# Value weights at group borders on GpSimd's DMA queue, in another order of steps; first-layer weight measures begun one block later and in other pieces

## The chip, the cores and the metric

The kernel runs on one core of a Trainium2 chip. Work that matters here is done by TensorE (PE in the profile; its weight loads are PEld), VectorE (DVE), ScalarE (ACT), GpSimd (POOL) and by DMAs, which SyncE's queue (SPq) or GpSimd's queue (POOLq) issues. Each engine works through its own list of instructions in order, and waits at an instruction until the semaphores that it needs have come. The metric is the device time of the kernel in microseconds (us), the median of several runs. The kernel's list of instructions for each engine is made by a scheduler that simulates the program on a time line while it is built: an instruction can be placed earlier than it stands in the source if its inputs are ready there, and `tc.issue_after(x)` keeps it from being placed ahead of `x`.

## What is computed

Two layers on a (1, 1024, 1024) float32 input. Layer 0 is an RG-LRU mixer (width 1536, in 12 blocks of 128), layer 1 a forgetting attention (16 heads of 64). Cut to what matters:

```python
x = x + lru_mixer(rms_norm(x, norm_g[0]), ...)
x = x + fox_mixer(rms_norm(x, norm_g[1]), fox_w_in, fox_b_f, fox_w_out)
return rms_norm(x, final_g)

def fox_mixer(h, w_in, b_f, w_out):
    u = h @ w_in                      # q, k, v, gate, forget logits
    cum = cumsum(log_sigmoid(f_logit + b_f))
    p = softmax(q k^T / 8 + cum_q - cum_k, causal)
    o = p @ v
    return (o * silu(gate)) @ w_out
```

## The kernel before

Matrix products are made of three passes with operands that are split into a high and a low part (fp32r in layer 0, fp16 in layer 1). Layer 1's fp16 parts need scales, so the squared norms of layer 1's weights have to be known before layer 1 begins. They are measured during layer 0.

**Layer 0** is the loop over 12 blocks (lines 472 to 524). A block `n` makes the input product `ups` of block n (lines 480 and 493), the gates of block n-1 (`gates`), the convolution (`conv`, DVE), the output products of earlier blocks (`project_out`, `fill`), the gate product `gps` of block n-1 (lines 511 to 516) and the recurrence (`recur`). The weights of `ups` and `gps` come through `weights`: SP loads them (tile `wf`), ACT casts the high part (`wh`), GpSimd subtracts to the low part (`wl`, line 114).

Between these stands `some()` (lines 466 to 469), nine times in a block: it takes one step of `squares_of_weights` (lines 419 to 442), which loads 256 KB of layer-1 weights on SP's queue into a tile `wsf` and has ACT square an earlier piece with a running sum (`measure`, lines 444 to 449). There are 81 pieces: 16 of `wv`, 48 of `w1`, 16 of `wo1`, one of `wf`. `wsf` shares two buffers with `wgf`, the raw gate weights that `conv` loads. It takes 82 steps to be through; block 2 is the first to take any, and so the steps end at the start of block 11. A piece of `wv` is measured in two halves of 128x256, since each of its two rows of `k` has its own column of `vsq`, which `weight_bounds` (line 600) multiplies by the squared gains of the norm. `largest_gain` (line 454) finds the largest squared gain: it is called in block 2 as a whole and holds one of the two PSUM buffers of the tag "O" from its first matmul to its last read. The gate products (line 339) take their PSUM tiles from the same tag.

**Layer 1** is a loop over 16 heads. For every group of four heads the values are projected by `values_beside` (16 steps, "v"), beside the attention of the group before. Their weights are made by `value_weights` (line 779, five steps, "w"): in a step it casts the piece that is there (ACT the high part, DVE the low part, tile `wv`) and loads the next of four pieces of 256 KB into the tile `wvf`, which has one buffer (line 792). Each load therefore waits until both casts of the piece before have read it. The load stands on SP's queue behind the last DMA transpose (line 793), among the transposes of the attention and the loads of T, U and `wf`.

The order of steps is written in strings that `run` (line 1127) plays: "." is a step of the projections (`fill`, six matmuls of 128x512), "0" a step of `weigh` (the product of attention and values), "1" a step of `maxima` (one row of scores S, softmax, transpose), "v" and "w" the steps above. A head plays two strings, `first` and `second` (lines 1359 to 1378). Group 1's value weights are made by the string in line 1332 and by START; those of groups 2 and 3 by TURN, in the second half of heads 3 and 7, and the heads after these, 4 and 8, play OPEN in their first half, in which the first values of the new group are made. All the value PSUM tiles (line 802) are of the tag "O", two buffers, which `weigh` uses too. When a head up to 11 is through, the rest of its projections is played at once (`drain(fill)`).

Of the kernel before, what the change touches and what calls it, by code (L numbers as in the profile page):

```python
# [11 lines left out]
F32 = mybir.dt.float32  # L12
# [3 lines left out]
TOP = 32768.0  # L16
AF = mybir.ActivationFunctionType
ALU = mybir.AluOpType

P = 128  # L20
SEQ = 1024
HALF = 512
KT = 8
# [3 lines left out]
EPS = 1e-6  # L27
GROUP = 2
ORDER = "1.v1..1.v1..00", "1.v1..1.v1..0000"
TURN = "w1v.v1w.w1..w1..w.0000"  # L30
OPEN = "1..1..1.v1.v00"
START = "1.w1.w1..1..00", "1v.1.v.1v.1v.0000"
LAST = "1..1..1..1..0.0", "1..1.1..1..0..0.0.0"
NEG = -1e30
# [9 lines left out]
def trunk(ctx: ExitStack, tc: tile.TileContext, xt, w0, wg, wo0, pc, gn, gf, w1, wv, wf, bf, wo1, out):  # L44
    nc = tc.nc
# [22 lines left out]
    def fetch(to, src):  # L68
        loaded_last[0] = loads_by[0].dma_start(to, src)  # L69

    def matmul(*args, **kw):
        pe[0] = nc.tensor.matmul(*args, **kw)  # L72
        return pe[0]
# [129 lines left out]
    with nullcontext(ExitStack()) as l0:  # L203
# [106 lines left out]
        def product(pt, h, w):  # L310
            gemm(pt, zip(w, raw[h]))
# [107 lines left out]
        def squares_of_weights():  # L419

            todo = [
                (wv[g, :, k : k + 2], [vsq[:, g, k + i : k + i + 1] for i in range(2)])
                for g in range(4)
                for k in range(0, KT, 2)
            ]
            todo += [(w1[b, :, 4 * j : 4 * j + 4], [wsq[:, 2 * b + j : 2 * b + j + 1]]) for b in range(24) for j in range(2)]
            todo += [(wo1[d, :, 4 * j : 4 * j + 4], [wsq[:, 48 + 2 * d + j : 49 + 2 * d + j]]) for d in range(KT) for j in range(2)]
            todo.append((wf, [root[:, 1:2]]))
            held = []
            for src, to in todo + [(None, None)]:  # L430
                if len(held) == 2 or src is None and held:
                    measure(*held.pop(0))
                if src is None:
                    break
                n = src.shape[1] * src.shape[2]
                wt = tmp.tile([P, HALF], F32, tag="wgf", name="wsf", bufs=2)[:, :n]
                nc.sync.dma_start(wt.rearrange("p (a b) -> p a b", b=src.shape[2]), src)
                held.append((wt, n // len(to), to))
                yield
            for h in held:  # L440
                measure(*h)
                yield
# [11 lines left out]
        def largest_gain():  # L454
            g2_ = root[:, 4:6]
            nc.vector.tensor_reduce(g2_[:, 0:1], gnt[:, 1], mybir.AxisListType.X, ALU.max)
            nc.vector.tensor_reduce(g2_[:, 1:2], gnt[:, 1], mybir.AxisListType.X, ALU.min)
            nc.vector.tensor_tensor(g2_, g2_, g2_, ALU.mult)
            nc.vector.tensor_tensor(g2_[:, 0:1], g2_[:, 0:1], g2_[:, 1:2], ALU.max)
            row = ps.tile([P, HALF], F32, tag="O", name="gmax")  # L460
            matmul(row[:1, :P], g2_[:, 0:1], ident, start=True, stop=True)
            nc.vector.tensor_reduce(root[:1, 6:7], row[:1, :P], mybir.AxisListType.X, ALU.max)
            matmul(row[:, P : P + 1], onesf[:1], root[:1, 6:7], start=True, stop=True)
            nc.vector.tensor_scalar(largest, row[:, P : P + 1], float(SEQ), 1e-20, ALU.mult, ALU.add)

        def some():
            if n > 1:
                with tc.issue_after(act[0].ins):
                    next(wsquares, None)

        ys, fill, held = [], iter(()), {}
        for n in range(NB):
            wu = first[0] if n == 0 else list(weights(w0[n]))
            if n == 1:
                ups = both = [ps.tile([P, HALF], F32, tag="g", name="ups") for h in range(2)]
            else:
                ups = two_banks("ups")
                both = [ups.rearrange("p a b -> p (a b)")]
                ups = [ups[:, h] for h in range(2)]
            product(ups[0], 0, wu)  # L480
            if n == 0:
                gps = held[0] = two_banks("gps")
                product(gps[:, 0], 0, first[1])
                for _ in zip(split_x(1), square_x(1)):
                    pass
                norm_row(0)
            else:
                gates(n - 1)
                if n > 1:
                    with tc.issue_after(state[n - 1]["last"].ins):  # L490
                        outputs(n - 2)
            some()
            product(ups[1], 1, wu)
            some()
            if n == 0:
                product(gps[:, 1], 1, first[1])
                norm_row(1)
            conv(n, both)
            some()
            if n == 0:  # L500
                with tc.issue_after(state[0]["tap"].ins):
                    softplus()
            if n % 2 and n > 1:
                fill = itertools.chain(fill, project_out((n - 3) // 2))
            take(fill, 2)
            some()
            take(fill, 2)
            some()
            if n == 2:
                largest_gain()  # L510
            if n > 1:
                wn = list(weights(w0[NB + n - 1]))
                gps = held[n - 1] = two_banks("gps")
                for h in range(2):
                    product(gps[:, h], h, wn)
                    some()
            if n:
                drain(silu(state[n - 1], held.pop(n - 1)))

                with tc.issue_after(state[n]["tap"].ins):  # L520
                    recur(n - 1)
                some()
            take(fill, 4)
            some()
# [2 lines left out]
        gps = two_banks("gps")  # L527
        for h in range(2):
            product(gps[:, h], h, wn)
        outputs(NB - 2)  # L530
        drain(fill)
        recur(NB - 1, halves)
# [21 lines left out]
        scale_v, unit_v = wsq[:, 88:92], wsq[:, 92:]  # L554
        rf = small.tile([P, 8], F32, name="rf")
        outs = small.tile([P, 8], F32, name="outs")
        total_o, unit_o, scale_o, scale_y, inv_o, eps_o, most = (outs[:, i : i + 1] for i in range(7))
        g2 = small.tile([P, KT], F32, name="g2")
        gx = [small.tile([P, KT], F32, name=f"gx{h}") for h in range(2)]
        xsq = [small.tile([P, KT], F32, name=f"xsq{h}") for h in range(2)]  # L560
# [39 lines left out]
        def weight_bounds():  # L600
# [2 lines left out]
            nc.vector.tensor_tensor(squared_bias, bft, bft, ALU.mult)  # L603
            matmul(all_[:, 64:128], onesf, wsq[:, :64], start=True, stop=True)
            matmul(all_[:, 160:161], onesf, root[:, 1:2], start=True, stop=True)
            matmul(all_[:, 32:64], onesf, vsq.rearrange("p a b -> p (a b)"), start=True, stop=True)
            nc.vector.tensor_tensor(g2, gnt[:, 1], gnt[:, 1], ALU.mult)
            nc.vector.tensor_tensor(vsq, vsq, g2.unsqueeze(1).to_broadcast([P, 4, KT]), ALU.mult)
            matmul(all_[:, :32], onesf, vsq.rearrange("p a b -> p (a b)"), start=True, stop=True)
            matmul(all_[:, 169:], onesf[:HEADS], squared_bias, start=True, stop=True)  # L610
            for cs, to, n in ((slice(0, 64), bounds[:, :8], KT), (slice(64, 112), bounds[:, 8:], 2)):
                nc.vector.tensor_reduce(
                    to, all_[:, cs].rearrange("p (a b) -> p a b", b=n), mybir.AxisListType.X, ALU.add
                )
            nc.vector.tensor_tensor(bounds[:, 4:5], bounds[:, 4:5], all_[:, 160:161], ALU.add)
            nc.vector.tensor_reduce(total_o, all_[:, 112:128], mybir.AxisListType.X, ALU.add)
            nc.scalar.activation(scale_v, bounds[:, :4], AF.Sqrt, bias=tiny, scale=SEQ / TOP / TOP)
            nc.scalar.activation(unit_w, bounds[:, 4:], AF.Sqrt, bias=tiny, scale=1.0 / TOP / TOP)
            nc.vector.reciprocal(scales, unit_w)
            nc.vector.tensor_scalar(unit_v, scale_v, 0.5 / TOP, None, ALU.mult)  # L620
# [75 lines left out]
    with ExitStack() as l1:  # L696
# [82 lines left out]
        def value_weights(g):  # L779
            raw, got = None, []  # L780
            for k in range(0, KT + 2, 2):
                if raw is not None:
                    both = at.tile([P, 2, 2, 256], FP16, tag="wv", name="wv", bufs=4)
                    hi, lo = both[:, 0], both[:, 1]
                    with tc.issue_after(seen[0].ins) if seen[0] else nullcontext():
                        nc.scalar.activation(hi, raw, AF.Copy, scale=scales[:, g : g + 1])
                    nc.vector.scalar_tensor_tensor(lo, raw, scales[:, g : g + 1], hi, ALU.mult, ALU.subtract)
                    got += [(hi[:, i], lo[:, i]) for i in range(2)]
                    if k > KT:
                        break  # L790
                if k < KT:
                    raw = at.tile([P, 2, 256], F32, tag="wvf", name="wvf", bufs=1)
                    with tc.issue_after(turns[-1].ins) if turns else nullcontext():
                        fetch(raw, wv[g, :, k : k + 2])
                else:
                    vw[g] = got
                yield
# [538 lines left out]
        for hd in range(HEADS):  # L1336
# [21 lines left out]
                fill = play(next(fills))  # L1358
            first, second = LAST if hd > 11 else START if hd == 0 else ORDER
            if hd in (4, 8):  # L1360
                first = OPEN
            if hd == HEADS - 1:
                first = "1..1.0.1.0.1..."
            side = chain(pieces(hd + 1, 0, 0), pieces(hd + 1, 0, 1)) if hd else iter(())
# [105 lines left out]
```

## Time and profile before

| | us |
|---|---|
| median of 3 runs | 1049.89 (1049.81 to 1050.67) |
| the profiled execution, its own time | 1047.91 |
| its span in the trace | 1046.2 |
| PE busy | 1006.5 |
| DVE busy | 802.3 |
| ACT busy | 676.8 |
| POOL busy | 103.2 |

The time of the profiled execution is 1.7 us more than its span and 2.0 us less than the median of the runs. PE is the engine with the most work, so the time is the work of PE plus the time in which PE stands still or runs at a lower clock; where that happens is read from windows along the span. Layer 0 takes the span up to about 445 us, the attention of layer 1 begins at about 520 us, and heads 4 and 8 begin at about 652 and 770 us.

### The profile page before, as it was taken

How to read it: one execution, taken by the hardware profiler on the slowest of the kernel's cores; microseconds unless marked ns; L12 is line 12 of the kernel's file. 1: busy time of each engine (PE TensorE's matmuls, PEld its weight loads, DVE VectorE, ACT ScalarE, POOL GpSimd, SP SyncE). 2: the span in 40 equal slices, each digit the busy share in tenths (PEclk: the TensorE clock that was granted, in tenths of full speed). 3: DMA queues.
4: the chain of work that ended last, by engine and by line, in shares of the span. 5: the costliest groups of instructions: out<-in, count | busy, mean ns of one | idle time of the engine just before them, and what ended most of it. 6: DMA issues, size and time to landing. Idle time of an engine off the chain costs nothing. (4 is left out here: it accounts for less than half of the span.)

```text
span 1046.2 us, 15137 instructions
## 1 busy us (share of the span) xinstructions
PE 1006.5 (96%) x5100; PEld 657.9 (63%) x5100; DVE 802.3 (77%) x1504; ACT 676.8 (65%) x1247; POOL 103.2 (10%) x90
## 2 busy tenths in 40 slices
PE   9998899999999999998899999899998999998997
PEld 7786677878888888866545555455544555444454
DVE  7787776486666659897686988888887978997765
ACT  8467776656666666455775666666666766774555
POOL 1312120211222111000300000000000000012100
PEclk9998999999999999999999999999999999999999
DMA  7112443342433331243465677777677777789964
GB/s 253 60 51 82 120 138 114 101 136 85 128 111 116 105 99 41 81 143 112 113 151 116 122 155 145 171 137 149 131 168 142 142 150 136 156 206 225 255 168 161
DMA packets 223037, 140.60 MB, mean 134 GB/s; under 512 B 162352, under 2 KB 188016, under 8 KB 222960
## 3 DMA queue, kind: packets, MB, share of 16 engines
q1 hardware_dynamic: 220560, 131.77, 52.1%
q0 software_dynamic: 2400, 7.87, 2.3%
q8 instruction: 40, 0.66, 0.3%
q14 instruction: 37, 0.30, 0.1%
HBM read 77.52 MB, written 11.73 MB: 85 GB/s over the span
## 5 line engine op out<-in xcount | busy, mean ns | idle before, releaser
L72 PE MATMUL gps<-h,w 128*128 128x512 f16 x1152 | 272.4, 383 | 2.8 <-DVE qkl L890 2.6
L72 PEld LDWEIGHTS <-w 128*128 128x128 f16 x1440 | 140.5, 98 | 160.8 <-issue 10.6
L60 ACT ACTIVATE p<-p,m 128x128 f32<-128x128 f32 (+7 forms) x128 | 98.8, 772 | 78.1 <-DVE m L1059 74.3
L1059 DVE CUSTOM_DVE_ANT_0 p<-S,mask,vsq 128x128 f32<-128x128 f32 (+7 forms) x128 | 103.8, 812 | 17.0 <-PE S L72 15.5
L1072 DVE SCALAR_TENSOR_TENSOR pp<-p,sums,pp 128x128 f16<-128x128 f32 (+7 forms) x128 | 103.6, 812 | 11.7 <-ACT pp L60 11.6
L114 POOL TENSOR_TENSOR wl<-wf,wh 128x512 fp32r<-128x512 f32 x46 | 80.6, 1755 | 323.6 <-ACT wh L60 265.8
L60 ACT ACTIVATE pp<-p,sums 128x128 f16<-128x128 f32 (+7 forms) x128 | 97.9, 768 | 20.9 <-ACT p L60 12.6
L72 PEld LDWEIGHTS <-h 128*128 128x128 f16 x768 | 74.6, 98 | 33.9 <-issue 9.4
L60 ACT ACTIVATE wsf<-wsf 128x512 f32<-128x512 f32 (+2 forms) x97 | 53.6, 554 | 48.7 <-DMA wsf<-in_w 22.2
L72 PE MATMUL S<-T,U 128*128 128x512 f16 (+4 forms) x384 | 83.9, 328 | 0.1
L72 PE MATMUL vps<-wv,h 128*128 128x256 f16 x576 | 72.1, 274 | 9.2 <-ACT wv L60 3.6
L72 PE MATMUL gps<-hh,wl 128*128 128x512 f32 x192 | 76.3, 397 | 4.4 <-POOL wl L114 4.4
L72 PE MATMUL gps<-hh,wh 128*128 128x512 f32 x192 | 76.6, 399 | 1.7 <-ACT wh L60 1.7
L72 PE MATMUL ups<-hh,wl 128*128 128x512 f32 x192 | 76.2, 397 | 1.7 <-POOL wl L114 1.7
L72 PE MATMUL ups<-hh,wh 128*128 128x512 f32 x192 | 77.0, 402 | 0.8 <-ACT hh L60 0.8
L72 PE MATMUL ops<-yh,wh 128*128 128x512 f32 x192 | 77.0, 401 | 0.5 <-DVE x L670 0.4
L72 PE MATMUL ops<-yh,wl 128*128 128x512 f32 x192 | 75.7, 394 | 1.1 <-DVE wl L114 1.1
L72 PE MATMUL ups<-hl,wh 128*128 128x512 f32 x192 | 76.6, 399 | 0.0
L72 PE MATMUL gps<-hl,wh 128*128 128x512 f32 x192 | 76.0, 396 | 0.0
L72 PE MATMUL ops<-yl,wh 128*128 128x512 f32 x192 | 74.8, 395 | 0.0
L408 DVE TENSOR_TENSOR x<-x,ops 128x512 f32<-128x512 f32 x80 | 53.9, 680 | 22.1 <-PE ops L72 21.7
L60 ACT CAST wh<-wf 128x512 fp32r<-128x512 f32 x72 | 43.4, 609 | 38.9 <-PE ops L72 24.8
(245 smaller groups left out, 1808.6 us busy)
## 6 DMA issues: line engine op xcount, KB each, us to landing
wf<-in_w SPq DMA_DIRECT2D x106, 256.0 KB
wsf<-in_w SPq DMA_DIRECT2D x48, 256.0 KB
wf<-in_wo SPq DMA_DIRECT2D x64, 128.0 KB
x<-in_xt SPq DMA_DIRECT2D x16, 256.0 KB
wsf<-in_wv SPq DMA_DIRECT2D x16, 256.0 KB
wsf<-in_wo SPq DMA_DIRECT2D x16, 256.0 KB
x1d<-x SPq DMA_DIRECT2D x16, 256.0 KB
T<-qkh SPq DMA_DIRECT2D x64, 64.0 KB
```

The costliest lines, as they stand in the source:

```text
L60: act[0] = op(*args, **kw)
L72: pe[0] = nc.tensor.matmul(*args, **kw)
L114: return eng.tensor_tensor(lo, src, f32(hi), ALU.subtract)
L408: nc.vector.tensor_tensor(x, x, pt, ALU.add)
L1059: nc.vector.tensor_tensor_reduce(p, S[:, :n], mask[:, SEQ - n :], unit_s[:, pair : pair + 1], -NEG, ALU.add, ALU.min, accum_out=m)
L1072: nc.vector.scalar_tensor_tensor(both[:, :, 1], p, r, both[:, :, 0], ALU.mult, ALU.subtract)
```

## The change

Five things are changed.

- `value_weights` issues its loads on GpSimd's queue, with no `issue_after`.
- TURN has the fourth and fifth "w" one "." earlier, and the third and fourth "1" one "." later. OPEN becomes a pair, for both halves of heads 4 and 8: in the first half both "v" stand behind the fourth "1", in the second half both are later than in ORDER.
- `some()` takes no step before block 3, and there are two more calls of it in the last gate product, behind the loop: 83 calls in all where there were 90.
- A piece of `wv` is measured whole, 128x512 at once, into one column; `weight_bounds` uses these sums with the largest gain in place of the gain of every row (a wider bound for the scale of the values), which takes away one product on PE and one on DVE.
- `largest_gain` is a generator in three steps, taken in blocks 3, 4 and 5.

```diff
-TURN = "w1v.v1w.w1..w1..w.0000"
-OPEN = "1..1..1.v1.v00"
+TURN = "w1v.v1w.w.1w..1w..0000"
+OPEN = "1..1..1..1vv.00", "1..1..1v.1v.0000"
...
-                (wv[g, :, k : k + 2], [vsq[:, g, k + i : k + i + 1] for i in range(2)])
+                (wv[g, :, k : k + 2], [vsq[:, g // 2, g % 2 * 4 + k // 2].unsqueeze(1)])
...
             nc.vector.tensor_tensor(g2_[:, 0:1], g2_[:, 0:1], g2_[:, 1:2], ALU.max)
+            yield
             row = ps.tile([P, HALF], F32, tag="O", name="gmax")
             matmul(row[:1, :P], g2_[:, 0:1], ident, start=True, stop=True)
             nc.vector.tensor_reduce(root[:1, 6:7], row[:1, :P], mybir.AxisListType.X, ALU.max)
+            yield
+            row = ps.tile([P, HALF], F32, tag="O", name="gmax")
             matmul(row[:, P : P + 1], onesf[:1], root[:1, 6:7], start=True, stop=True)
...
+        gains = largest_gain()
+
         def some():
-            if n > 1:
+            if n > 2:
...
-            if n == 2:
-                largest_gain()
+            if n > 2:
+                next(gains, None)
...
         for h in range(2):
             product(gps[:, h], h, wn)
+            some()
         outputs(NB - 2)
...
-            matmul(all_[:, 32:64], onesf, vsq.rearrange("p a b -> p (a b)"), start=True, stop=True)
+            matmul(all_[:, 48:64], onesf, flat[:, :16], start=True, stop=True)
             nc.vector.tensor_tensor(g2, gnt[:, 1], gnt[:, 1], ALU.mult)
-            nc.vector.tensor_tensor(vsq, vsq, g2.unsqueeze(1).to_broadcast([P, 4, KT]), ALU.mult)
-            matmul(all_[:, :32], onesf, vsq.rearrange("p a b -> p (a b)"), start=True, stop=True)
+            nc.vector.tensor_scalar(gain, largest, 1.0 / TOP / TOP, None, ALU.mult)
...
-            nc.scalar.activation(scale_v, bounds[:, :4], AF.Sqrt, bias=tiny, scale=SEQ / TOP / TOP)
+            nc.scalar.activation(scale_v, bounds[:, 4:8], AF.Sqrt, bias=tiny, scale=gain)
...
-                    with tc.issue_after(turns[-1].ins) if turns else nullcontext():
-                        fetch(raw, wv[g, :, k : k + 2])
+                    nc.gpsimd.dma_start(raw, wv[g, :, k : k + 2])
...
             if hd in (4, 8):
-                first = OPEN
+                first, second = OPEN
```

More of the change, by code (lines that the diff above doesn't have):

```diff
@@ L556, in trunk @@
         outs = small.tile([P, 8], F32, name="outs")
-        total_o, unit_o, scale_o, scale_y, inv_o, eps_o, most = (outs[:, i : i + 1] for i in range(7))
+        total_o, unit_o, scale_o, scale_y, inv_o, eps_o, most, gain = (outs[:, i : i + 1] for i in range(8))
         g2 = small.tile([P, KT], F32, name="g2")
@@ L605, in weight_bounds @@
             matmul(all_[:, 160:161], onesf, root[:, 1:2], start=True, stop=True)
-            matmul(all_[:, 32:64], onesf, vsq.rearrange("p a b -> p (a b)"), start=True, stop=True)
+            matmul(all_[:, 48:64], onesf, flat[:, :16], start=True, stop=True)
             nc.vector.tensor_tensor(g2, gnt[:, 1], gnt[:, 1], ALU.mult)
-            nc.vector.tensor_tensor(vsq, vsq, g2.unsqueeze(1).to_broadcast([P, 4, KT]), ALU.mult)
-            matmul(all_[:, :32], onesf, vsq.rearrange("p a b -> p (a b)"), start=True, stop=True)
+            nc.vector.tensor_scalar(gain, largest, 1.0 / TOP / TOP, None, ALU.mult)
             matmul(all_[:, 169:], onesf[:HEADS], squared_bias, start=True, stop=True)
-            for cs, to, n in ((slice(0, 64), bounds[:, :8], KT), (slice(64, 112), bounds[:, 8:], 2)):
+            for cs, to, n in ((slice(48, 64), bounds[:, 4:8], 4), (slice(64, 112), bounds[:, 8:], 2)):
                 nc.vector.tensor_reduce(
```

## The prediction

> **What bounds the kernel now.** I read the page first.
>
> ```profile
> span 1046.2 us, 15137 instructions
> PE 1006.5 (96%) x5100; PEld 657.9 (63%) x5100; DVE 802.3 (77%) x1504; ACT 676.8 (65%) x1247; POOL 103.2 (10%) x90
> ```
>
> PE leaves 1046.2 - 1006.5 = 39.7 us of the span unused. The change takes almost nothing off PE's own work, so its worth must lie in those 39.7 us and in a low clock. Windows of 15 us along the span show where they are (length; busy time of PE, PEld, DVE, ACT and POOL; granted clock, DMA share, GB/s):
>
> ```profile
> 90.00:105.00 15.00, 10.59 (x40) 8.05 (x39) 9.30 (x8) 7.66 (x25) 5.89 (x1) 0.77 0.40 121
> 105.00:120.00 15.00, 13.63 (x59) 10.77 (x58) 10.04 (x8) 14.78 (x30) 3.09 (x2) 1.00 0.32 95
> 255.00:270.00 15.00, 15.00 (x66) 12.18 (x65) 13.07 (x15) 10.71 (x20) 5.78 (x2) 1.00 0.50 158
> 390.00:405.00 15.00, 15.00 (x67) 12.19 (x66) 14.34 (x15) 8.24 (x13) 2.58 (x2) 1.00 0.13 36
> 540.00:555.00 15.00, 12.37 (x74) 7.13 (x73) 12.30 (x31) 9.61 (x19) 0.00 (x0) 0.89 0.92 186
> 660.00:675.00 15.00, 12.03 (x70) 6.61 (x70) 11.29 (x27) 11.36 (x20) 0.00 (x0) 0.89 0.71 179
> 780.00:795.00 15.00, 11.42 (x73) 6.46 (x72) 13.07 (x31) 10.82 (x21) 0.00 (x0) 1.00 0.85 155
> ```
>
> Four holes lie where the change works: block 2 of layer 0 (4.4 us in the window at 90) and the three group borders (2.6, 3.0 and 3.6 us); in three of them the clock falls too. The window at 255, in a block that carries nine measures, has none: PE is full. So a microsecond of PE's idle time saved in a hole is one off the end. What ends PE's waits there (total, times, longest):
>
> ```profile
> PE gps L72 <- POOL wl L114: 4.4, 1, 4.4
> PE vps L72 <- DVE v L774: 3.9, 5, 1.9
> PE vps L72 <- ACT wv L60: 3.6, 3, 2.2
> PE vps L72 <- DVE wv L787: 1.9, 2, 1.5
> ```
>
> GpSimd's low part is the wait in layer 0; the value products (`vps`) wait for their own weights and for their PSUM.
>
> **Block 2 of layer 0.** From the timeline:
>
> ```profile
> 83.43 0.42 ACT L60 ACTIVATE wsf<-wsf 128x256 f32<-128x256 f32 x1
> 85.75 0.43 ACT L60 ACTIVATE wsf<-wsf 128x256 f32<-128x256 f32 x1
> 86.82 1.21 DVE L316 TENSOR_TENSOR us<-ups,rs 128x1024 f32<-128x1024 f32 x1
> 89.59 0.50 PE L72 MATMUL gps<-hh,wh 128*128 128x512 f32 x1 [0.52 <-ACT wh L60]
> 89.62 6.27 POOL L114 TENSOR_TENSOR wl<-wf,wh 128x512 fp32r<-128x512 f32 x1 [15.44 <-ACT wh L60]
> 94.76 0.12 DVE L464 TENSOR_SCALAR root<-gmax 128x1 f32<-128x1 f32 x1
> 95.94 0.80 PE L72 MATMUL gps<-hh,wl 128*128 128x512 f32 x1 [4.41 <-POOL wl L114]
> 99.41 0.40 PE L72 MATMUL gps<-hh,wh 128*128 128x512 f32 x1
> 105.42 1.29 POOL L114 TENSOR_TENSOR wl<-wf,wh 128x512 fp32r<-128x512 f32 x1 [9.53 <-ACT wh L60]
> 112.30 0.50 PE L72 MATMUL ups<-hh,wl 128*128 128x512 f32 x1 [1.37 <-POOL wl L114]
> ```
>
> GpSimd's subtraction takes 1.29 us at 105.42 and 6.27 at 89.62, beside a busy DVE, and it started late because ACT made `wh` late. The change takes the measures out of this block, and the gain's steps, with L464 and the PSUM buffer that they hold until 94.76. Two pieces are measured between 83.43 and the cast, each two halves of 0.43: 1.7 us. Without them the subtraction starts at about 87.9, beside L316 (86.82 to 88.03), whose first operand is in PSUM. I take it at its usual length there, and the waits of 0.52 and 4.41 as gone. The clock comes back with them: the eight matmuls begun from 95.94 to 99.41 take 3.47 us, at the full window's pace (15.00 / 66 = 0.23) 1.84; that is 1.6. Together **-6.5 us**. At the other end 0: DVE may hold GpSimd as long at another place.
>
> The moved work comes back in block 3: first measures, first gain step. There PE already waits 1.37 (row at 112.30), with ACT 14.78 of 15 busy. I add one more wait of that size, **+1.4**, between 0 and the 4.4 of the old hole; it is nearer to the row of that block. The measures that now fill block 11, and the two behind it, meet ACT at 8.24 of 15 and DMAs at a share of 0.13 (window at 390): 0, hidden by PE's products, as in the window at 255. Were that cover gone, layer 1's scales would come late by one block's nine measures at most, 9 x 0.86 = 7.7 us. Whole pieces, the dropped product and smaller reductions are off PE's path: 0; they could bring some tenths at the change of layers.
>
> **The borders.** The chain is load, ACT's cast, DVE's cast, which frees the one buffer, next load; four times. From the timeline of the three borders; then a window near the end, where GpSimd's queue loads `xp`, and landing times on that queue (`xp`'s, then those of the issues of `xh`):
>
> ```profile
> 535.63 0.72 ACT L60 ACTIVATE wv<-wvf,wsq 128x512 f16<-128x512 f32 x1 [1.20 <-DMA wvf<-in_wv]
> 549.19 0.75 DVE L787 SCALAR_TENSOR_TENSOR wv<-wvf,wsq,wv 128x512 f16<-128x512 f32 x1 [0.34 <-ACT wv L60]
> 648.60 0.72 ACT L60 ACTIVATE wv<-wvf,wsq 128x512 f16<-128x512 f32 x1 [1.74 <-DMA wvf<-in_wv]
> 654.56 0.75 DVE L787 SCALAR_TENSOR_TENSOR wv<-wvf,wsq,wv 128x512 f16<-128x512 f32 x1
> 657.72 0.52 SPq L69 DMA_DIRECT2D wvf<-in_wv  x1
> 661.24 0.72 ACT L60 ACTIVATE wv<-wvf,wsq 128x512 f16<-128x512 f32 x1 [2.20 <-DMA wvf<-in_wv]
> 663.39 1.46 PE L72 MATMUL gps<-h,w 128*128 128x512 f16 x6
> 666.71 0.38 PE L72 MATMUL vps<-wv,h 128*128 128x256 f16 x2 [1.20 <-ACT wv L60]
> 667.75 0.74 DVE L787 SCALAR_TENSOR_TENSOR wv<-wvf,wsq,wv 128x512 f16<-128x512 f32 x1
> 668.55 0.60 PE L72 MATMUL vps<-wv,h 128*128 128x256 f16 x4 [1.47 <-DVE wv L787]
> 670.87 2.36 PE L72 MATMUL gps<-h,w 128*128 128x512 f16 x6
> 766.76 0.72 ACT L60 ACTIVATE wv<-wvf,wsq 128x512 f16<-128x512 f32 x1 [2.02 <-DMA wvf<-in_wv]
> 784.93 0.75 DVE L787 SCALAR_TENSOR_TENSOR wv<-wvf,wsq,wv 128x512 f16<-128x512 f32 x1
> 790.71 1.49 PE L72 MATMUL vps<-wv,h 128*128 128x256 f16 x12 [1.88 <-DVE v L774]
> 930.00:945.00 15.00, 15.00 (x77) 7.01 (x76) 13.88 (x31) 11.48 (x21) 2.16 (x4) 1.00 0.98 253
> DMA to landing us min/median/max: 3.1/4.2/5.7
> xh<-x1d POOLq DMA_DIRECT2D x4, 256.0 KB, 7.6
> ```
>
> On SP's queue a free buffer isn't filled at once: free at 654.56 + 0.75 = 655.31, loaded from 657.72, 2.4 later. GpSimd's queue is empty in this part of the span (POOL 0.00 in the windows from 540 on), and with no transpose to stay behind, a group's first piece can land long before its step. At 4.2 us a load (the median of the nearest rows; ends 3.1 and 7.6) a round is 4.2 + 0.72 + 0.75 = 5.7, three are 17.0, and the last two casts take 1.5, or 2.6 if DVE comes to the last one as late as now (667.75, when ACT was done by 666.71).
>
> - Second border: the first cast no longer waits 1.74, so it can start at 646.9; 646.9 + 17.0 + 1.5 to 2.6 gives 665.4 to 666.5, against 668.5 now. Of PE's 1.20 + 1.47 some 2.2 go. The six matmuls at 670.87 take 2.36 against 1.46 at 663.39: 0.9 of clock goes too. **-3.1.**
> - Third: 764.7 + 18.5 to 19.6 gives 783.2 to 784.3, against 785.7: of the hole's 3.6 the part before the third value step (3.6 - 1.9) shrinks by 1.2. That step's own 1.88 waits for the first value tile to be read out of PSUM; OPEN now puts it behind three rows of S instead of one. I take 1.5 of it. **-2.7.**
> - First, whose strings stay: the second cast can come 1.20 sooner, at 534.4; two rounds and 1.5 give 547.3 against 549.9, the whole hole of 2.6 at best, nothing if the casts stay where ACT's and DVE's lists have them now. I take **-1.0**, and leave its clock (0.89 in the window) as it is.
>
> The "v" moved later in OPEN cost PE nothing: the second one stands behind as many "1" and "." as before. What waits on GpSimd's queue behind a load is another load. Twelve issues fewer on SP's queue (0.52 each) let transposes go sooner; PE waits for none there: 0.
>
> **Sum.** -6.5 + 1.4 - 3.1 - 2.7 - 1.0 = -11.9. Off the profiled execution's 1047.91 that is 1036.0; that execution is 2.0 under the median of the runs, so off 1049.89 the forecast is **1038.0 us**. With every term at its good end (block 3 at 0, border holes and clocks all gone) it is about 1033.
>
> **Rivals.** About 0.2%, 2.1 us, is what a measurement of this kernel tells from no change.
>
> 1. One half only: block 3 inherits block 2's hole (6.5 against up to 4.4 + 1.6), or the casts keep their places. Then 5.1 or 6.8 us are had: 1042 to 1047.7. For it speaks that the scheduler places every instruction anew, in which a gain can get lost; against it that the waits in both halves have plain causes that the change takes away. 0.26.
> 2. It doesn't do what it says: both halves keep their waits (a cast behind the same ACT list, DVE holding GpSimd elsewhere). 1047.8 to 1052. 0.13.
> 3. Slower: loads on GpSimd's queue land late. Nine loads lie in the chains, three a border, so the sum is -11.9 + 9 x (L - 4.2): it turns at L = 5.5 us, gives 1051.5 at 5.7, and 1069 at 7.6. Against it speaks that the `xp` loads landed in 4.2 with DVE busy for 13.88 of 15 us (window at 930), as here; for it that four `xh` loads in a row took 7.6. 1052 to 1069. 0.17.
>
> The Trainium skill speaks for this rival: "SBUF — State Buffer", section "SBUF: two separate sides", says that DVE, in certain modes, keeps GpSimd from the port through which it writes the descriptors of its DMAs, so that they stand still, and advises SP's or ACT's queue instead. The 6.27 us subtraction agrees that GpSimd can be held off by DVE; the 4.2 us landings do not show it for DMAs. By that rule the third rival's 1069 would be the time.
>
> My forecast, 1033 to 1041, has 0.44. Its range and those of rivals 1 and 2 hold 0.83: 1033 to 1052. Faster by over 0.2%: 0.44 + 0.26 = 0.70; within: 0.13; slower: 0.17.
>
> **What would show it.** Right, if `gps` waits for `wl` under 1 us in block 2 and the clock there is 1.00; if the first `wv` cast at the second and third border waits for no load, and the loads are issued within 0.5 us of the DVE cast that frees the buffer; if `vps` waits for `wv` under 1 us. Wrong, if POOL rows in blocks 2 or 3 are again above 5 us, if `wvf` lands later than 5.5 us after its issue, or if PE waits at the change of layers (435 to 450) grow.

## The result, and the profile after

The changed kernel takes 1033.66 us, the median of 4 runs (1030.52 to 1035.15), beside 1050.21 for the kernel before (4 runs, 1049.81 to 1050.67). The ratio is 0.9838, with a 95% interval of 0.9814 to 0.9863. The forecast was 1038.0 in a range from 1033 to 1052. The profiled execution of the changed kernel takes 1032.8, 15.1 less than that of before; the sum of the prediction was -11.9.

The head of the page of the changed kernel, in the order of the lines shown of before:

```profile
span 1030.9 us, 15125 instructions
...
PE 1002.0 (97%) x5098; PEld 656.4 (64%) x5098; DVE 797.4 (77%) x1504; ACT 674.7 (65%) x1215; POOL 104.1 (10%) x102
```

PE's unused time has gone from 39.7 us to 28.9 (1030.9 - 1002.0), and its busy time by 4.5: it has two matmuls less, so most of that must be the clock. Windows of the changed kernel (length; busy time of PE, PEld, DVE, ACT and POOL; granted clock, DMA share, GB/s), at the four holes of before and at two places where new ones have come up:

```profile
90.00:105.00 15.00, 13.10 (x55) 9.73 (x54) 14.42 (x15) 14.63 (x19) 2.08 (x1) 1.00 0.28 79
135.00:150.00 15.00, 12.51 (x49) 9.21 (x48) 9.64 (x11) 10.82 (x19) 2.54 (x2) 0.94 0.43 127
540.00:555.00 15.00, 15.00 (x95) 9.08 (x93) 12.79 (x37) 11.71 (x24) 0.54 (x1) 1.00 0.78 161
660.00:675.00 15.00, 15.00 (x96) 8.24 (x94) 12.97 (x36) 11.68 (x26) 0.00 (x0) 1.00 0.73 146
780.00:795.00 15.00, 15.00 (x97) 8.84 (x96) 11.56 (x29) 9.59 (x19) 0.00 (x0) 1.00 0.71 148
930.00:945.00 15.00, 11.01 (x49) 4.56 (x49) 6.30 (x19) 4.06 (x9) 3.23 (x6) 0.89 0.95 221
```

The windows at the three borders are full, at the full clock; a wait of 1.50 for a transpose, at 538.33, lies ahead of the first of them. What ends PE's waits now (total, times, longest):

```profile
PE O L72 <- DMA pT<-pp: 5.5, 3, 3.9
...
PE ups L72 <- ACT wh L60: 2.1, 1, 2.1
...
PE ups L72 <- POOL wl L114: 1.4, 2, 1.2
...
PE vps L72 <- DVE v L779: 0.4, 2, 0.3
```

`vps` no longer waits for `wv` at all, and `gps` no longer for `wl`. From the timeline of the changed kernel, block 2 and 3 and then the second border; behind them the landing times of the tile `wvf`:

```profile
87.67 1.51 POOL L114 TENSOR_TENSOR wl<-wf,wh 128x512 fp32r<-128x512 f32 x1 [13.85 <-ACT wh L60]
87.94 1.21 DVE L316 TENSOR_TENSOR us<-ups,rs 128x1024 f32<-128x1024 f32 x1
104.58 0.50 PE L72 MATMUL ups<-hh,wl 128*128 128x512 f32 x1 [1.19 <-POOL wl L114]
637.19 0.70 ACT L60 ACTIVATE wv<-wvf,wsq 128x512 f16<-128x512 f32 x1
638.19 0.73 DVE L792 SCALAR_TENSOR_TENSOR wv<-wvf,wsq,wv 128x512 f16<-128x512 f32 x1
639.22 0.54 POOL L798 DMA_DIRECT2D wvf<-in_wv  x1 [95.92 <-DVE v L779]
642.63 0.72 ACT L60 ACTIVATE wv<-wvf,wsq 128x512 f16<-128x512 f32 x1 [0.46 <-DMA wvf<-in_wv]
656.16 2.78 PE L72 MATMUL vps<-wv,h 128*128 128x256 f16 x24
656.54 0.74 DVE L792 SCALAR_TENSOR_TENSOR wv<-wvf,wsq,wv 128x512 f16<-128x512 f32 x1
667.00 1.47 PE L72 MATMUL vps<-wv,h 128*128 128x256 f16 x12
...
DMA to landing us min/median/max: 3.4/4.0/4.4
```

The first cast waits for no load, a load is issued 0.3 after the cast that frees the buffer (638.19 + 0.73 = 638.92, issued at 639.22), and the 24 matmuls of the first value tile run through.

**Where the time came from.** Every head runs its 16 products of attention and values in one go in its second half; the time from one head's to the next head's is 28.16 us wherever nothing stands in the way. Two such rows of before, heads 3 and 4, are 33.40 apart:

```profile
650.22 2.44 PE L72 MATMUL O<-pT,v 128*128 128x512 f16 x16
683.62 2.44 PE L72 MATMUL O<-pT,v 128*128 128x512 f16 x16
```

The same rows give the borders of every kernel in the table: border 2 shows from head 3 to 4, border 3 from 7 to 8. "S" is the start of the first scores, all that lies ahead of the attention. The first border shows from S to head 1's products. The expectations below count it from head 0 to head 1 instead, 34.20 before and 31.62 changed, but PE waits for nothing in that stretch in either kernel. Three rows show what differs there, two of before and one of the changed kernel:

```profile
549.21 0.38 PE L72 MATMUL vps<-wv,h 128*128 128x256 f16 x2 [2.22 <-ACT wv L60]
562.07 6.22 PE L72 MATMUL gps<-h,w 128*128 128x512 f16 x28
...
557.63 3.63 PE L72 MATMUL gps<-h,w 128*128 128x512 f16 x16
```

Before's wait for the weights comes ahead of head 0's products (559.70), so it isn't in that stretch. Behind these products stand 28 matmuls of the projections before and 16 in the changed kernel, where the scheduler put twelve of them ahead; twelve take 2.59 in before's chain, and that is the 2.58. The ratio is to the kernel before on the same chip.

| kernel | S | S to head 1 | border 2 | border 3 | median (ratio, 95%) |
|---|---|---|---|---|---|
| before | 519.68 | 74.22 | 33.40 | 32.70 | |
| changed | 515.59 | 71.28 | 28.16 | 28.50 | 1033.66 (0.9838, 0.9814 to 0.9863) |
| e1, layer 0 only | 514.63 | 73.51 | 33.06 | 32.36 | 1043.25 (0.9948, 0.9923 to 0.9973) |
| e2, borders only | 519.33 | 71.45 | 28.15 | 28.16 | 1038.01 (0.9896, 0.9859 to 0.9933) |
| e3, queue only | 523.19 | 71.40 | 31.94 | 31.72 | 1047.70 (0.9994, 0.9968 to 1.0021) |
| e4, strings only | 518.87 | 72.29 | 29.95 | 30.80 | 1044.22 (0.9949, 0.9916 to 0.9983) |
| e5, measures later only | 510.80 | 72.30 | 33.44 | 33.81 | 1041.96 (0.9931, 0.9903 to 0.9959) |
| e6, gain in steps only | 519.61 | 74.29 | 33.23 | 32.90 | 1049.39 (0.9997, 0.9975 to 1.0019) |
| e7, one low part on DVE | 517.69 | 73.49 | 33.44 | 32.76 | 1046.14 (0.9966, 0.9945 to 0.9987) |
| e8, changed, SP's queue, not held | 512.26 | 75.02 | 28.64 | 28.28 | 1035.69 (0.9881, 0.9843 to 0.9919) |
| e9, measures later and borders | 512.27 | 71.18 | 28.16 | 28.77 | 1031.06 (0.9839, 0.9810 to 0.9867) |
| e10, changed once more | 512.18 | 71.36 | 28.16 | 28.29 | 1030.66 (0.9824, 0.9798 to 0.9850) |
| e11, changed, held on GpSimd's queue | 513.16 | 71.48 | 28.16 | 28.16 | 1030.27 (0.9825, 0.9797 to 0.9853) |
| e12, changed, old OPEN | 513.58 | 71.16 | 32.72 | 35.05 | 1043.07 (0.9955, 0.9931 to 0.9978) |

Between the two profiled executions S came 4.1 sooner, the three borders gave 2.9, 5.2 and 4.2, and behind head 8's products 1.2 were lost: 15.3 of span. S is a loose column: the changed kernel has it at 515.59 in one execution and at 512.18 in another (e10). The borders of the two are within 0.3 of each other. What comes behind head 8's products is not in the table and is as loose: no edit changes a step there, yet it takes 245.4 in before, the shortest of the 14 profiled executions, 246.6 in the changed kernel, and up to 252.3 (e4).

### The profile page after: what moved, and what is told of

It is laid out like the page before. It is cut to its first block, busy times and chain, and to the rows that moved or that the text cites. A ratio compares the mean times of both kernels' runs of the same rounds, so it can differ in the third digit from the quotient of the medians.

```text
span 1030.9 us, 15125 instructions
## 1 busy us (share of the span) xinstructions
PE 1002.0 (97%) x5098; PEld 656.4 (64%) x5098; DVE 797.4 (77%) x1504; ACT 674.7 (65%) x1215; POOL 104.1 (10%) x102
## 5 line engine op out<-in xcount | busy, mean ns | idle before, releaser
L72 PE MATMUL gps<-h,w 128*128 128x512 f16 x1152 | 268.3, 379 | 3.3 <-DVE qkl L894 2.7
L60 ACT ACTIVATE p<-p,m 128x128 f32<-128x128 f32 (+7 forms) x128 | 98.8, 772 | 72.3 <-DVE m L1063 67.1
L114 POOL TENSOR_TENSOR wl<-wf,wh 128x512 fp32r<-128x512 f32 x46 | 74.9, 1634 | 328.9 <-ACT wh L60 271.6
L60 ACT ACTIVATE wsf<-wsf 128x512 f32<-128x512 f32 (+1 forms) x81 | 50.6, 626 | 51.8 <-DMA wsf<-in_w 26.3
L72 PE MATMUL ops<-y,w 128*128 128x512 f16 x288 | 68.9, 386 | 0.9 <-DVE sg L1032 0.7
```

Source lines behind the costliest of these rows:

```text
L60: act[0] = op(*args, **kw)
L114: return eng.tensor_tensor(lo, src, f32(hi), ALU.subtract)
```

## The experiments

### The two halves alone (e1, e2)

e1 has only the layer 0 edits (`some()` from block 3, whole pieces of `wv`, the wider bound, the gain in steps), e2 only those of the borders (queue, TURN, OPEN).

> The layer-0 part of the change alone (measures from block 3, whole pieces of wv, the largest gain in three steps, the new bounds); value weights and strings as before. My theory (each hole has its own cause, and the parts add): block 2's hole of 4.4 us is gone, as in the changed kernel the attention begins 4.1 us earlier (first S at about 515.6 instead of 519.7), and the borders keep their losses: heads 1, 4 and 8 end their second O product 34.2, 33.4 and 32.9 us after the head before, where an undisturbed head takes 28.2. Time about 4 us under the kernel before. Rival (the two halves hang together through the scheduler): more than 6 us, or the borders change as well.

> The border part alone (loads on GpSimd's queue, new TURN and OPEN), layer 0 as before. My theory: first S at 519.7 as before, 4.4 us of idle PE in the window 90 to 105 stay; head 1, 4 and 8 intervals fall to about 31.6, 28.2 and 28.5; time about 11 to 12 us under the kernel before, so that this and the layer-0 part add up to the change. Rival: the borders need the earlier layer 0, and this gives under 8.

Layer 0 alone gives 0.9948 and the borders alone 0.9896. Their product is 0.9845, against 0.9838 for both: they add up. The borders are worth about twice as much as layer 0; the prediction had 6.8 and 5.1.

### The borders: queue or strings (e3, e4)

```diff
# e3, before with this alone
-                    with tc.issue_after(turns[-1].ins) if turns else nullcontext():
-                        fetch(raw, wv[g, :, k : k + 2])
+                    nc.gpsimd.dma_start(raw, wv[g, :, k : k + 2])
# e4, before with this alone
-TURN = "w1v.v1w.w1..w1..w.0000"
-OPEN = "1..1..1.v1.v00"
+TURN = "w1v.v1w.w.1w..1w..0000"
+OPEN = "1..1..1..1vv.00", "1..1..1v.1v.0000"
```

> Only the twelve loads move to GpSimd's queue; TURN and OPEN as before, layer 0 as before. My theory: the chain of casts gets earlier, which takes the waits for wv at all borders (2.6, 2.7 and 1.7 us) and the low clock after them at the first and second; the third value step still waits for its PSUM at the third border (1.88 before), since OPEN is the old one. Intervals 31.6, 28.5 and 30 to 31; time 8 to 10 us under before. Rival A (the strings do it): under 3 us. Rival B (GpSimd's queue is slower): slower than before.

> Only the strings TURN and OPEN change, the loads stay on SP's queue behind the transposes. My theory: the last wv cast ends about as late as before (some 1 us earlier at most), so the second value step still waits 1 to 3 us for it and the clock falls after it; the third step's wait for its PSUM (0.3 and 1.88 us) goes. First border untouched, 34.2. Second 32 to 33.4, third 31 to 32; time 1 to 4 us under before. Rival A (the strings do it): intervals of 28.2 to 28.5 at heads 4 and 8, about 9 us under before.

The queue alone gives the first border what the whole change gives it (71.40 from S to head 1; its strings stay), and takes 1.5 and 1.0 off the others; the strings alone are not played at the first border, and take 3.5 and 1.9 off the others. In the timeline of e3 (GpSimd in block 2, then PE at the second and third border):

```profile
88.90 10.27 POOL L114 TENSOR_TENSOR wl<-wf,wh 128x512 fp32r<-128x512 f32 x1 [15.44 <-ACT wh L60]
94.46 1.26 DVE L320 SCALAR_TENSOR_TENSOR xc<-us,pct,xc 128x1022 f32<-128x1022 f32 x1
99.23 0.79 PE L72 MATMUL gps<-hh,wl 128*128 128x512 f32 x1 [8.40 <-POOL wl L114]
667.61 0.60 PE L72 MATMUL vps<-wv,h 128*128 128x256 f16 x4 [1.39 <-DVE wv L787]
672.77 1.47 PE L72 MATMUL vps<-wv,h 128*128 128x256 f16 x12 [2.07 <-DVE sums L1068]
783.80 0.60 PE L72 MATMUL vps<-wv,h 128*128 128x256 f16 x4 [1.17 <-DVE wv L787]
788.97 1.47 PE L72 MATMUL vps<-wv,h 128*128 128x256 f16 x12 [2.07 <-DVE sums L1068]
```

At the second border the wait for the weights is 1.39 where it was 1.20 + 1.47, but the third value step, which begins the second value tile, waits 2.07 where it waited 0.31: what the queue gives, that step takes back. In e4 the third value step waits for nothing, and the weights are still late (timeline of e4, second border: the last load, its casts, PE):

```profile
659.12 0.54 SPq L69 DMA_DIRECT2D wvf<-in_wv  x1
662.88 0.72 ACT L60 ACTIVATE wv<-wvf,wsq 128x512 f16<-128x512 f32 x1 [2.02 <-DMA wvf<-in_wv]
663.65 0.38 PE L72 MATMUL vps<-wv,h 128*128 128x256 f16 x2 [1.07 <-ACT wv L60]
664.43 0.60 PE L72 MATMUL vps<-wv,h 128*128 128x256 f16 x4 [0.41 <-DVE wv L787]
```

So there are two waits in a row, and each half of the change cures one. That the whole of e3 shows no gain (0.9994) although its borders gain 5 us is in part the first three lines: S comes 3.5 later than in before. In the profiled execution the stretch behind head 8's products takes 3.6 longer, too. By the code nothing in layer 0 differs; GpSimd's subtraction was held 10.27 instead of 6.27 there, which is taken up below.

### OPEN taken back (e12)

```diff
# the changed kernel with
-OPEN = "1..1..1..1vv.00", "1..1..1v.1v.0000"
+OPEN = "1..1..1.v1.v00"
...
-                first, second = OPEN
+                first = OPEN
```

> The changed kernel with the old OPEN (the new TURN kept). Theory A (the prediction's step): OPEN only moves the third value step behind the read-out of the first value tile, so the second border stays near 28.2 and the third loses up to 1.5 (near 30.0). Theory B: OPEN's later values are what covers the last casts, so both borders lose 1 to 2 us, near 29.5 and 30.

Both borders lose far more than either theory had: 32.72 and 35.05, which is 4.6 and 6.8 over the changed kernel e10, measured on the same chip, and the third is worse than before the change. From the timeline of e12:

```profile
655.34 1.47 PE L72 MATMUL vps<-wv,h 128*128 128x256 f16 x12
661.23 0.37 ACT L60 ACTIVATE v<-vps,rv 128x128 f16<-128x128 f32 x1
661.24 0.74 DVE L1110 SCALAR_TENSOR_TENSOR yo<-O,wsq,yo 64x512 f32<-64x512 f32 x1
661.96 0.34 DVE L779 SCALAR_TENSOR_TENSOR v<-vps,rv,v 128x128 f16<-128x128 f32 x1
662.03 1.85 PE L72 MATMUL vps<-wv,h 128*128 128x256 f16 x12 [2.71 <-DVE sums L1073]
780.77 2.72 PE L72 MATMUL vps<-wv,h 128*128 128x256 f16 x12 [4.26 <-DVE sums L1073]
```

The weights are there, and the first tile is through (655.34 is its second half). But both buffers of the tag "O" are full then: the first value tile has one, and the product of attention and values that follows it has the other. Both are read out behind the softmax in ACT's and DVE's lists, some 5 us later, and the third value step has to wait for one of them. It began at 662.03, just after the read of the attention product ended (L1110, 661.24 + 0.74 = 661.98) and before that of the value tile did (L779, 661.96 + 0.34 = 662.30), so it was the product's buffer that it took. (The profile names L1073, which stands between the two in DVE's list. In before, the read-out of `v` is the one that ends the wait.) In the changed kernel the value tile is read out just as late, the second half at 664.90 in the timeline below, but the third value step comes later still, at 667.00:

```profile
661.27 2.75 PE L72 MATMUL gps<-h,w 128*128 128x512 f16 x12
664.08 2.75 PE L72 MATMUL gps<-h,w 128*128 128x512 f16 x12
664.90 0.33 DVE L779 SCALAR_TENSOR_TENSOR v<-vps,rv,v 128x128 f16<-128x128 f32 x1
```

OPEN has 24 matmuls of the projections stand there instead. A part of what the hole costs is the clock: of the 4.6 at the second border 2.71 are idle, and most of the rest is slower matmuls (12 in 1.85 instead of 1.47 right behind the wait; the granted clock is 0.89 in the window from 660 to 675, which is 0.11 x 15 = 1.65 us).

### The queue, or the place behind a transpose (e8, e11)

```diff
# e8, the changed kernel with SP's queue, not held
-                    nc.gpsimd.dma_start(raw, wv[g, :, k : k + 2])
+                    fetch(raw, wv[g, :, k : k + 2])
# e11, the changed kernel with GpSimd's queue, held as before
-                    nc.gpsimd.dma_start(raw, wv[g, :, k : k + 2])
+                    with tc.issue_after(turns[-1].ins) if turns else nullcontext():
+                        nc.gpsimd.dma_start(raw, wv[g, :, k : k + 2])
```

> The changed kernel with its loads of value weights on SP's queue again, but free of the order behind the last transpose: the early first load is kept, the separate queue is not. My theory: on SP's queue a load that waits for its buffer either holds up the transposes behind it or stands behind them, so the loads are issued up to 2.4 us after their buffer is free; with the new strings there are some 2 us of slack, so the second and third border cost 0 to 2 us each (intervals 28.2 to 30.2), the first about 33 to 34.2; time 2 to 6 us over the changed kernel. Rival (only the early first load and the strings count, the queue does not): all intervals as in the changed kernel, time within 1 us of it.

> The changed kernel, loads of the value weights on GpSimd's queue but kept behind the last transpose when the lists are made, as before. Theory A, what counted was that a load is no longer put behind a transpose in the list: the second and third border come back to what the strings alone left (30.0 and 30.8 from head to head, first border near 34.2), ratio about 0.990. Theory B, what counted was that SP's queue works in order, and GpSimd's is empty: the borders stay within 0.5 us of the changed kernel's 31.6, 28.2 and 28.5, ratio about 0.984.

Held or not, GpSimd's queue gives the same borders (71.48 from S to head 1, then 28.16 and 28.16), with a load 0.3 behind its cast (654.38 + 0.75 = 655.13; timeline of e11):

```profile
654.38 0.75 DVE L792 SCALAR_TENSOR_TENSOR wv<-wvf,wsq,wv 128x512 f16<-128x512 f32 x1
655.43 0.54 POOL L799 DMA_DIRECT2D wvf<-in_wv  x1 [6.45 <-DVE wv L792]
```

On SP's queue, not held, borders 2 and 3 come within 0.5 of the changed kernel. Held there with the new strings (e4) they were 29.95 and 30.80. So what delays a load at these two borders is a place behind a transpose in a queue that works in order; either way out of it does. At the first border the two ways differ: from S to head 1 e8 takes 75.02 us, 3.7 more than the changed kernel and more than before, so that nothing is gained there. It shows ahead of head 0's products (42.55 us from S, 512.26 to 554.81, against 39.66), and a part of it is a wait for a transpose (timeline of e8; the changed kernel waits 1.50 there); how the loads on SP's queue bring it about was not followed up:

```profile
537.17 1.69 PE L72 MATMUL O<-pT,v 128*128 128x512 f16 x8 [2.91 <-DMA pT<-pp]
```

The whole of e8, 0.9881 (0.9843 to 0.9919), cannot be told from the changed kernel's 0.9838 (0.9814 to 0.9863).

### Layer 0: which of its edits (e5, e6, e7)

```diff
# e5, before with this alone
-            if n > 1:
+            if n > 2:
...
             product(gps[:, h], h, wn)
+            some()
# e6, before with largest_gain in three steps in blocks 3, 4 and 5
-            if n == 2:
-                largest_gain()
+            if n > 2:
+                next(gains, None)
...
# e7, before with the low part of block 2's gate weights made by DVE
-                wn = list(weights(w0[NB + n - 1]))
+                wn = list(weights(w0[NB + n - 1], lo_eng=nc.vector if n == 2 else nc.gpsimd))
```

> Kernel before, with the measures begun in block 3 (and the two steps behind the loop), pieces of wv still in halves, the largest gain still as a whole in block 2. My theory: the hole of block 2 is there because ACT, held up by the measures, makes wh late, so that GpSimd's subtraction starts when DVE already runs operations with two SBUF inputs one behind the other. Without the measures it starts near 87.9, beside the operation that reads PSUM, and takes about 1.5 us: hole gone, first S 4 to 5 us earlier than in the kernel before, time about 4 us less. Rival (the gain's steps and their PSUM buffer make the hole): it stays at 4 us or more.

> Kernel before, with only the largest gain moved, in three steps over blocks 3 to 5; the measures begin in block 2 as before. My theory: wh is as late as before and the subtraction starts near 89.6 again, but now DVE has not even the two short reads of PSUM (L462, L464) in which GpSimd could come in: it is held until DVE's list runs dry, near 99; a hole of 4 to 9 us, first S 0 to 5 us later than in the kernel before. Rival (the gain's steps make the hole): hole gone, about 4 us faster.

> Kernel before, with only the two low parts of block 2's gate weights (two 128x512 subtractions) made by VectorE in place of GpSimd. Measures the hold-off by itself. My theory: DVE does each in about 0.67 us, in its list, within 2 us after wh; the wait of 4.4 for wl becomes at most 2, the clock in the window 90 to 105 rises from 0.77 to 1.00, first S about 4 us earlier. Rival (DVE is simply late with all its work, GpSimd's share is no matter): wl ends near 95 again and the wait stays at 4.

The later measures alone give all that layer 0 gives (0.9931, against 0.9948 for its whole half), and the gain in steps gives nothing (0.9997). In the timeline of e5, GpSimd's subtraction is where it is in the changed kernel, although L464 still reads the gain in block 2; the window at 135 is full, where the changed kernel's is not:

```profile
87.76 1.51 POOL L114 TENSOR_TENSOR wl<-wf,wh 128x512 fp32r<-128x512 f32 x1 [13.84 <-ACT wh L60]
96.80 0.14 DVE L464 TENSOR_SCALAR root<-gmax 128x1 f32<-128x1 f32 x1
...
135.00:150.00 15.00, 15.00 (x66) 12.03 (x65) 7.23 (x8) 7.76 (x23) 4.57 (x2) 1.00 0.51 158
```

In e6 the measures stay in block 2, the subtraction starts late as before, and this time it is held 2.75 (timeline of e6):

```profile
88.58 2.75 POOL L114 TENSOR_TENSOR wl<-wf,wh 128x512 fp32r<-128x512 f32 x1 [15.44 <-ACT wh L60]
90.21 2.21 DVE L320 SCALAR_TENSOR_TENSOR xc<-us,pct,xc 128x1023 f32<-128x1023 f32 x1
91.39 0.50 PE L72 MATMUL gps<-hh,wl 128*128 128x512 f32 x1 [0.94 <-POOL wl L114]
102.61 0.49 PE L72 MATMUL ups<-hh,wh 128*128 128x512 f32 x1 [1.44 <-ACT wh L60]
109.57 0.50 PE L72 MATMUL ups<-hh,wh 128*128 128x512 f32 x1 [1.39 <-ACT wh L60]
```

The hole is 0.94 instead of 4.41, yet nothing is gained: PE meets waits for ACT's casts in block 3, which still carries its nine measures. e7 says the same from the other side. It takes GpSimd out of the 4.41 altogether and gains 3.8 us (1049.96 to 1046.14), some of which comes back as waits a block later: its window at 120 has PE busy for 12.41 of 15 us, that of before 13.74. The measures' move has the best median of the three (0.9931, against 0.9966 and 0.9997), as one would expect if ACT's lateness is the cause; but its interval overlaps that of e7.

### Measures and borders without the rest (e9, e10)

e9 is the kernel before with e5's edit and the borders: without whole pieces, the wider bound and the gain in steps. e10 is the changed kernel on the same chip.

> The kernel before with two parts of the change: no measures before block 3 (two more calls behind the loop), and the whole borders half (GpSimd's queue, TURN, OPEN). Left out: whole pieces of wv, the wider bound, the gain in three steps. Theory A, those three parts are worth nothing or a little less: the measures alone began S at 510.8 where the changed kernel did at 515.6, mostly because PE was full from 135 to 150 us (15.00 of 15 against 12.51). If that and the borders add up, ratio 0.993 x 0.990 = 0.983, 1031 to 1034 us, borders at 31.6, 28.2 and 28.2 to 28.5 from head to head. Theory B, the three parts are needed for the full gain: ratio above 0.987, S not before 515.

> The changed kernel itself, beside the run that leaves three of its parts out, on the same chip. Ratio 0.984 as before, if nothing differs by chip.

1031.06 and 1030.66 us, with overlapping intervals: the three parts left out in e9 are worth nothing that can be measured. With e11 (1030.27) there are three forms of the change here, and none beats another.

## Why the prediction was right, and where it was not

**The sum.** -11.9 was forecast and -15.1 came between the profiled executions; between the medians it was -16.6. The direction held, and so did the waits that were to go; the borders were mis-sized. The median, 1033.66, lies only 0.7 above the lower end of the range, for which every term had to come out at its good end, and the same kernel on another chip (e10, 1030.66) lies below that end.

**Block 2, -6.5: right.** The subtraction was to start at about 87.9 and to run at its usual length beside L316. It started at 87.67 and took 1.51, not 1.29; both waits are gone, and the clock in the window at 90 is 1.00. From the start of its first matmul to that of its last the block's gate product took 15.0 us (84.22 to 99.25) instead of 21.9 (84.88 to 106.80): 6.9. One reason was wrong: the gain's steps, and the PSUM buffer that they hold, have no share in it (e5, e6).

**Block 3, +1.4: not there, and too small.** `ups` waits 1.4 in all for `wl` (longest 1.2), but it waited 1.7 before (longest 1.37, in the same block): no second wait of that size was added. The moved work costs PE at the next place, 2.1 us for a cast of ACT in the window at 135, with a clock of 0.94 (0.06 x 15 = 0.9 us): 3.0. Together with block 2's 6.9 that is about the 4.1 by which S moved in one profiled execution; over both, the start of S moved by 4.1 and 7.5, around the 5.1 of the prediction.

**First border, -1.0: too small.** From S to head 1 2.9 came. The waits of 2.22 and 0.41 for the weights are gone: the casts did not stay where the lists had them, and DVE's last one began at 541.72 instead of 549.19. A new wait of 1.50 for a transpose took back a part, and a wait ahead of these, 2.64 at 522.81 in before, no longer falls into this stretch. But the clock in the window at 540, which the prediction left at 0.89, is 1.00: 1.65 us. How much of the 2.9 is the queue's is known only roughly: the seven kernels with their loads on GpSimd's queue take 71.2 to 71.5 from S to head 1, and the six that have them on SP's queue, held, take 72.3 to 74.3, although these six do not differ in the border's own steps.

**Second border, -3.1: the step that was wrong.** 5.2 came. The prediction gave it all to the queue, 2.2 of the 1.20 + 1.47 and 0.9 of clock. The queue alone gave 1.5 (e3): of the waits for the weights 1.3 went, and the third value step took 1.8 back; what it gained came from the clock, 0.89 before and 1.00 in e3 in the window from 660 to 675 (1.65 us). That step's wait was booked at the third border only, at 1.5, because in the trace of before it is 0.31 at the second. But 0.31 was what remained of it behind 2.7 us of waiting for weights. With the weights in time and the old OPEN it is 2.71 and 4.26 (e12), and with the clock 4.6 and 6.8 a border. The prediction asked what is late next after the weights, and read the answer off a trace in which the first wait still covered the second. That OPEN, which it brought in for the third border, was there to mend the second as well was luck: by its account the queue would have been enough. Of the 2.1 us by which the term is short, 0.5 are waits for the weights, 0.3 the third value step's, and 0.75 the clock (1.65 where 0.9 was taken, below).

**Third border, -2.7: too small.** 4.2 came. In before the waits ahead of the third value step were 0.15 + 1.54 = 1.69, of which the prediction took 1.2; the step's own was 1.88, of which it took 1.5. Both went in full, and some 0.6 of what the border lost beside its waits. The queue alone took only 1.0 off (e3), since the third step's wait grew to 2.07 there, as at the second border.

**The clock.** At the second border the prediction took 0.9, from six matmuls. The granted clock was 0.89 over the 15 us of the window at 660, which is 1.65; the slow matmuls go on past the six that were counted. The head was 33.40 long where 28.16 is undisturbed, and its waits in PE were 1.20 + 1.47 + 0.31 = 2.98; with the clock that makes 4.6 of 5.24, and no row names the rest. Idle time alone does not set the price: in e3 the same border has 1.39 + 2.07 = 3.46 of waits, a clock of 1.00, and loses 3.78.

**Costed at nothing.** The moved "v" did cost PE nothing, and the measures at the end of layer 0 were hidden. Behind head 8's products the changed kernel lost 1.2 us to before, and e2 2.7. The changed kernel waits 3.9 for a transpose there, in the window at 930; before waits 3.0 for the same product, at 951.09. It is not settled why.

**The rivals.** One half only and no effect are out by e1 and e2. The third, slower, is out by its own turning point: it needed 5.5 us from a load's issue to its landing on GpSimd's queue, and the twelve took 3.4 to 4.4. The rule of the Trainium skill that was weighed there, "SBUF — State Buffer", section "SBUF: two separate sides", speaks of certain modes of DVE. DVE was busy for 11.6 to 13.0 of 15 us in the windows of the borders, and no load on GpSimd's queue stood still; in which modes DVE worked there, no row tells. That DVE can hold off GpSimd itself agrees with the 10.27 us of e3.

## What to carry to other kernels

Where two waits follow each other on one engine, the second one's length in the trace is what the first has left of it; work out when its input is ready by itself, from the lists of the engines that make it, before crediting the first one's cure in full. A load on an in-order queue can be late because of what it stands behind: here taking it out from behind that and giving it an empty queue came to the same at two borders, and only the empty queue helped at the first. When two traces are compared from mark to mark, count the work between the marks: a stretch without a single wait got 2.6 us shorter here because twelve matmuls had moved out of it. Of the five edits here, the queue and OPEN carry the borders and the later measures carry layer 0; what TURN gives by itself was not measured.

## What was not expected of the hardware

GpSimd's subtraction of 128x512 took 1.51, 2.75, 6.27 and 10.27 us in block 2 of different kernels; where it began beside DVE's list, and a few small instructions of that list, differ between them. In before it ended (89.62 + 6.27 = 95.89) within this instruction of DVE, which took 1.26 in e3:

```profile
94.81 2.16 DVE L320 SCALAR_TENSOR_TENSOR xc<-us,pct,xc 128x1022 f32<-128x1022 f32 x1
```

In e6 it got through beside the L320 before that one, again stretched, to 2.21. In e3 the L320 at 94.46 took 1.26, and GpSimd was not through until 99.17, some 4 us later (rows above). So the same code in layer 0 gave a hole of 4.4 and one of 8.4 us; what decides it at that instruction is left open. It may be one source of the spread of the kernel before, 1042.31 to 1054.38 in 25 runs on one chip; that was not tested, and the stretch behind head 8's products is another place where executions differ.
